# The first inverse moved among the last projections, and a hand-written order for TensorE in the recurrence stage

## The chip, the cores and the metric

One core of one Trainium2 chip runs the kernel. The metric is device time in microseconds (us) of one execution. Profile and trace come from one execution that the hardware profiler recorded.

## The reference, cut to what matters

Two transformer blocks on 512 tokens of width 1024. The change lies in the first block, whose mixing part has two branches on the same normalised input: a gated delta rule with 8 heads of 64 features, worked in chunks, and a sliding-window attention with 8 query heads.

```python
A = jnp.where(strict, jnp.einsum('bhncd,bhnsd->bhncs', kb, k) * decay, 0.0)
L = A + jnp.eye(CHUNK, dtype=A.dtype)
sol = lax.linalg.triangular_solve(L, rhs, left_side=True, lower=True, unit_diagonal=True)
u, w = sol[..., :Dv], sol[..., Dv:]
qk = jnp.where(causal, jnp.einsum('bhncd,bhnsd->bhncs', q, k) * decay, 0.0)
...
def step(S, inp):
    u_c, w_c, qk_c, qd_c, kd_c, dec_c = inp
    v_new = u_c - jnp.einsum('bhcd,bhde->bhce', w_c, S)
    o = jnp.einsum('bhcd,bhde->bhce', qd_c, S) + jnp.einsum('bhcs,bhse->bhce', qk_c, v_new)
    S = S * dec_c[..., None, None] + jnp.einsum('bhcd,bhce->bhde', kd_c, v_new)
    return S, o
```

After the mixing come the output projection, a feed-forward part, and a second block with four branches; the change does not touch them.

## The kernel before

Features lie on partitions for the projections (weights split into a high and a low float32r part, three matmuls for one product, `mm3`, L302), tokens for the rest. The kernel works the delta rule in 4 chunks of 128 tokens; a chunk is a block `b`, the heads go by parity `e`, so a tile `[P, 512]` holds the four heads of one parity.

The stage that the change is about runs after the queries, keys and values of the delta rule. Its parts:

- **Last projections.** `proj(19 + j)` (four query tiles of the attention) and `gate_z(p)` (L919, four gate tiles), 24 dense 128x512 matmuls each.
- **Inverse of a chunk** (`inverse`, L775). From the inverses of 16x16 diagonal blocks (`block_inverse`, L749) it doubles the block size twice. For each parity there are four products of whole 128x128 matrices, four heads each: L804 and L809 for blocks of 16, L818 and L824 for blocks of 32. VectorE masks or subtracts after the first two, ScalarE copies the kept parts after the last two. It also forms the decayed scores (L796, contraction over 64 partitions). In the trace a float32 matmul is two records, so a product of four heads is eight.
- **Recurrence of a chunk** (`recur`, L847). Keys times state (L836 in `state_product`), then the inverse applied by halves with 64x64 matmuls (L864, L869, L872), then the new state (L880). After each of them VectorE or ScalarE forms the next operand.
- **Outputs of a chunk** (`outputs`, L891). Queries times state (L836), scores times new values (L900), a norm on VectorE and ScalarE, transposes (L916).
- **Attention.** Eight units (4 blocks x 2 key heads). `swa_scores` (L1002): score matmuls L1012, softmax on VectorE and ScalarE. `swa_values` (L1038): transposes L1047, copies on ScalarE, value matmuls L1051.
- **Modulation vectors.** `adaln2` (L366) loads weights on SP's queue, multiplies on ScalarE and adds on GpSimd, then transposes on TensorE (L380) and sums on ScalarE. Two of the six groups stand in this stage.

What sets the order: a planner sorts each engine's instructions by priority and its own estimate of when they are ready. The program gives the turns (L31) and raises the priority of inverse, recurrence and outputs:

```python
TURNS = (0, 0, 1, 1, 0, 2, 1, 2, 3, 2, 3, 3)
...
    with tc.high_priority(offset=1000):
        done = next(steps[b], "done") == "done"
```

Engines take their instructions in the planned order, and an instruction that waits holds those behind it. PSUM has eight banks (L239): here 0, 1, 2 for the inverse, 4 for the recurrence, 5 for the outputs, 3 and 7 for attention scores and transposes, 6 for attention values and the modulation vectors.

Earlier, `conv_silu` (L603) takes twelve projection tiles through a causal convolution: ScalarE copies the tile from PSUM to SBUF (L607), scales it once more from PSUM (L610), and VectorE adds the three other taps from the SBUF copy (L612).

Of the kernel before, what the change touches and what calls it, by code (L numbers as in the profile page):

```python
# [16 lines left out]
P = 128  # L17
T = 512
# [10 lines left out]
ADA_AT = (2, (3, 4), (3, 6))  # L29
# [21 lines left out]
# column offsets in the packed table of per-feature vectors  # L51
# [9 lines left out]
# columns of the constant table  # L61
# [32 lines left out]
def _rope():  # L94
    """rows 0-63 ones, 64-95 cos, 96-127 signed sin, for the 528 positions; then the row map of the key rotation."""
    inv = (1.0 / (10000.0 ** (np.arange(0, 32, 2, dtype=np.float32) / np.float32(32)))).astype(np.float32)
    ang = np.arange(TM, dtype=np.float32)[None, :] * inv[:, None]
    cos, sin = np.cos(ang).astype(np.float32), np.sin(ang).astype(np.float32)
    t = np.zeros((P, TM + P), np.float32)
    t[:64, :TM] = 1.0  # L100
    t[64:96, :TM] = np.concatenate([cos, cos])
    t[96:, :TM] = np.concatenate([-sin, sin])
    i = np.arange(32)
    for a_ in (64, 96):
        for b_ in (64, 96):
            t[a_ + i, TM + b_ + i] = 1.0
    return t


def _pack(inp):  # L110
# [13 lines left out]
    # shift1 | scale1 by feature tile, then the other four by 512 columns  # L124
# [87 lines left out]
class Halves:  # L212
    """a weight chunk [P, 8, 128] kept as two tiles [P, 512]"""
# [9 lines left out]
def build(ctx, tc, A, out):  # L223
    nc = tc.nc
    V, S, G, E = nc.vector, nc.scalar, nc.gpsimd, nc.tensor
# [71 lines left out]
    def mm3(dst, w, wk, x, first=True, last=True):  # L297
        """dst += W^T x over the k-tiles: wk are positions in the weight chunk, x the (hi, lo) operands."""
# [14 lines left out]
    def gemv(how, acc, views, after=None):  # L313
        """acc [P, n] = sum over the k-tiles of weights times silu(c); by VectorE, or ScalarE and GpSimd."""
# [18 lines left out]
    def early_slots():  # L333
        """tiles [P, 512] in space that is free until the projections are under way"""
# [15 lines left out]
    def adaln1(k, how, raws, after=None):  # L350
        """shift1 and scale1 of feature tile k"""
# [14 lines left out]
    def adaln2(g, how, ring):  # L366
        """modulation tiles 16 + 4g to 19 + 4g"""
# [9 lines left out]
        gemv(how, acc, views)  # L377
        pt = psum("sm")
# [6 lines left out]
        V.tensor_tensor(out=mod[:, c:c + 4], in0=mod[:, c:c + 4], in1=vec[:, VEC["b_ada"] + c:VEC["b_ada"] + c + 4], op=ALU.add)  # L385

# [5 lines left out]
    def rsqrt(t, w, sfx=""):  # L392
        """t <- t^-0.5 in place, t a 2D [p, w] view: bit-level first guess and three Newton steps."""
# [15 lines left out]
    def rms_stat(tiles, n, width=T, scratch=work):  # L409
        """rstd with tokens on partitions, [P, blocks], and the last matmul on its way"""  # L410
# [17 lines left out]
    def rms_spread(rs, width=T):  # L428
        """rstd by token along the free axis on all partitions, [P, width] in PSUM"""
# [10 lines left out]
    def modulated(xt, bc, w, sh, sc, hh, hl):  # L440
        """h = x*rstd*w*(1+scale)+shift for one feature tile, split."""
# [63 lines left out]
    def spare_w(i):  # L505
        """weights in the slots that the scores take later"""
# [21 lines left out]
    def tr4(src, dst):  # L528
        """transpose the four 128x128 blocks of src [P, 512] into the PSUM tile dst."""
# [45 lines left out]
    # decays to the end of the chunk: of the keys, and of the state by parity of the head  # L575
# [7 lines left out]
    # G along the free axis on all partitions, by way of DRAM  # L583
# [19 lines left out]
    def conv_silu(i, ct_, dst):  # L603
        """projection tile i -> causal conv (channel tile ct_) -> silu, into dst [P, 512]."""
        pt = proj(i)
        raw = xtile(turn[0] % 2)
        S.activation(out=raw, in_=pt, func=AF.Copy)  # L607
# [3 lines left out]
        for j in (1, 2, 3):  # L611
            V.scalar_tensor_tensor(out=y[:, j:T], in0=raw[:, 0:T - j], scalar=wj(3 - j), in1=y[:, j:T],  # L612
# [10 lines left out]
    def kstat(pt, dst, scale):  # L623
        """dst [P, NB, 2] = (sum of squares per head * scale + eps)^-0.5, from PSUM with tokens on partitions."""
# [16 lines left out]
    def head_sums(src, dst, p):  # L641
        """sums of squares of the heads 2p and 2p + 1 into dst [P, (chunk head)]"""
# [13 lines left out]
    def key_scales():  # L656
        """rk: sums of squares, the factor beta / sum, and the norm"""
# [7 lines left out]
    def key_rows(p):  # L665
        """keys by token, decayed to the end of the chunk"""
# [33 lines left out]
    rot = {"n": 0}  # L700

    def tmp_tile(b):
        if b == 0:
            return work()
        rot["n"] += 1
        return htile(f"l{4 + rot['n'] % 4}")
# [19 lines left out]
    def key_products(b, e):  # L726
        """at = Gram products of the keys times factor and decay; their 32x32 diagonal blocks to c32 [P, (chunk head), 32]"""
# [21 lines left out]
    def block_inverse():  # L749
        """x16 [P, (chunk head), 16]: the inverses of the 16x16 diagonal blocks by substitution, columns on partitions."""  # L750
# [6 lines left out]
        # sel[:, j]: row j of every block for all rows of the block  # L757
# [16 lines left out]

    def inverse(b):  # L775
        """Zi[b, e] = transpose of (I + A)^-1 for heads 2q + e, by doubling the block size; qkT[b, e] the decayed scores.
        Yields between the steps, so that two chunks can take turns."""
        at, x = {}, {}
        s = slice(b * P, (b + 1) * P)
        cs = [slice(q * P, (q + 1) * P) for q in range(4)]  # L780
        for e in range(2):
            i = 2 * (b % 2) + e
            o = 64 * e
            dt = qkT[b, e]
            at[e] = Zf[b, e]
            z = Zi[b, e] = (xtile(6 + e) if b == 0 else htile(f"h{i}") if b == 1 else
                            htile(f"h{e}") if b == 2 else gp.tile([P, T], F32, tag="Z", name="Z", bufs=8))
# [3 lines left out]
            x[e] = (gs.tile([P, T], F32, tag="vn", name="x", bufs=2) if b == 0 else  # L791
                    htile(f"h{4 + i}" if b < 2 else f"l{i}"))
# [939 lines left out]
```

## Time and profile before

| | us |
|---|---|
| median of 3 runs | 1276.18 |
| lowest and highest | 1273.61, 1287.78 |
| the profiled execution, first to last instruction (span) | 1298.0 |

The profiled execution is longer than each of the timed runs although its span leaves out what lies around the instructions. TensorE's granted clock, over the whole span, was 0.965 of full speed. The last projections end and the stage of inverse, recurrence and attention takes over near 216 us of the span; the output projection starts at 351 us, and the recurrence of the last chunk runs on among its products to 386 us.

How to read the rows: times are us from the start of the span. A stage's row has the busy time of PE (TensorE matmul), PEld (its weight loads), DVE (VectorE), ACT (ScalarE) and POOL (GpSimd), and the granted clock of TensorE as a share of full speed (1.00 is 2.4 GHz, 0.50 is 1.2 GHz).

### The profile page before, as it was taken

To read this page: it belongs to the slowest core of one execution; us is meant where nothing else is said; L and a number is where in the kernel's file an instruction comes from. 1 tells how busy PE (TensorE), PEld (TensorE's weight loads), DVE (VectorE), ACT (ScalarE), POOL (GpSimd) and SP (SyncE) were. 2 spreads that over 40 slices of the span, in tenths; PEclk is the share of its full clock that TensorE was granted. 3 is DMA by queue.
4 is the path that set the end of the run, shared out by engine and by line. 5 is a ranking of instruction groups with operands and counts; after the bars stand their busy time and mean duration, and the time that the engine had idled before them with its cause. 6 is when DMAs were issued, how large, how long until landed. Compare 5 with 4: busy or idle time off the path is not lost.

```text
span 1298.0 us, 17212 instructions
## 1 busy us (share of the span) xinstructions
PE 1253.2 (97%) x6470; PEld 1034.5 (80%) x6470; DVE 827.1 (64%) x1694; ACT 542.6 (42%) x1098; POOL 118.8 (9%) x99
## 2 busy tenths in 40 slices
PE   4989999999999999999999999999999999999997
PEld 4767778767799888888888889888888888788876
DVE  7789989554766643334433336798778876754554
ACT  5467733544635332222232223444444454432341
POOL 3450334310000000000000000012000000000000
PEclk9899999765999999999999999899999999999999
DMA  9545433210231423333233335122222222232441
GB/s 356 181 127 155 138 97 106 90 33 17 66 99 50 165 95 98 97 98 97 87 104 106 106 110 152 49 76 88 69 78 82 62 81 78 65 106 94 137 144 49
DMA packets 52627, 132.63 MB, mean 102 GB/s; under 512 B 6560, under 2 KB 14272, under 8 KB 52544
## 3 DMA queue, kind: packets, MB, share of 16 engines
q1 hardware_dynamic: 49472, 126.21, 30.8%
q10 hardware_dynamic: 3072, 5.33, 1.2%
q8 instruction: 51, 0.84, 0.3%
q14 instruction: 32, 0.26, 0.1%
HBM read 127.30 MB, written 4.21 MB: 101 GB/s over the span
## 4 chain that ended last, share of the span: by engine, by line
PE 82%; DVE 10%; DMA 5%; ACT 2%; issue 1%; POOL 0%; SPq 0%; DVEq 0%; ACTq 0%; POOLq 0%
PE ps_mm L302 56%; PE ps_out L302 4%; DVE x L612 2%; PE ps_ff L302 2%; DMA ada<-in_ada 2%; PE ps_po L1051 1%; PE ps_swa L1012 1%; PE ps_sc L1545 1%; DVE wlo L284 1%; PE ps_o L1575 1%; DMA raw<-in_wo 1%; PE ps_mm L1690 1%; PE ps_mm L1691 1%; PE ps_tr L1569 1%; PE ps_mm L1689 1%
## 5 line engine op out<-in xcount | busy, mean ns | idle before, releaser
L283 ACT ACTIVATE whi<-raw 128x1024 fp32r<-128x1024 f32 x141 | 147.3, 1045 | 268.9 <-PE ps_mm L302 206.2
L284 DVE TENSOR_TENSOR wlo<-raw,whi 128x1024 fp32r<-128x1024 f32 x140 | 170.9, 1221 | 94.9 <-ACT whi L283 94.6
L302 PE MATMUL ps_mm<-uh,whi 128*128 128x512 f32 (+1 forms) x544 | 197.3, 363 | 0.0
L302 PE MATMUL ps_mm<-uh,wlo 128*128 128x512 f32 (+1 forms) x544 | 196.7, 362 | 0.5 <-DVE work L1279 0.4
L302 PE MATMUL ps_mm<-ul,whi 128*128 128x512 f32 (+1 forms) x544 | 195.4, 359 | 0.0
L302 PE MATMUL ps_mm<-mh,whi 128*128 128x512 f32 x320 | 126.3, 395 | 0.0
L302 PE MATMUL ps_mm<-mh,wlo 128*128 128x512 f32 x320 | 125.2, 392 | 0.3 <-DVE wlo L284 0.3
L302 PE MATMUL ps_mm<-ml,whi 128*128 128x512 f32 x320 | 125.5, 392 | 0.0
L302 PEld LDWEIGHTS ps_mm<-ul,whi 128*128 128x128 f32 x544 | 102.5, 188 | 15.7 <-issue 0.7
L302 PEld LDWEIGHTS ps_mm<-uh,wlo 128*128 128x128 f32 x544 | 102.3, 188 | 15.8 <-DVE work L1279 0.7
L302 PEld LDWEIGHTS ps_mm<-uh,whi 128*128 128x128 f32 x544 | 102.3, 188 | 15.7 <-issue 1.5
L302 PEld LDWEIGHTS ps_mm<-ml,whi 128*128 128x128 f32 x320 | 60.0, 188 | 14.2
L302 PEld LDWEIGHTS ps_mm<-mh,wlo 128*128 128x128 f32 x320 | 60.0, 188 | 14.1 <-DVE wlo L284 0.4
L302 PEld LDWEIGHTS ps_mm<-mh,whi 128*128 128x128 f32 x320 | 59.9, 187 | 13.4
L302 PE MATMUL ps_mm<-ah,whi 128*128 128x512 f32 x176 | 69.8, 396 | 0.0
L302 PE MATMUL ps_mm<-ah,wlo 128*128 128x512 f32 x176 | 69.8, 396 | 0.0
L302 PE MATMUL ps_mm<-al,whi 128*128 128x512 f32 x176 | 69.8, 396 | 0.0
L302 PE MATMUL ps_mm<-hh,wlo 128*128 128x512 f32 x144 | 59.2, 411 | 0.6 <-ACT x L969 0.4
L329 POOL TENSOR_TENSOR acc<-acc,ada 128x512 f32<-128x512 f32 (+1 forms) x42 | 51.3, 1222 | 87.7 <-ACT ada L328 74.4
L302 PE MATMUL ps_mm<-hl,whi 128*128 128x512 f32 x144 | 59.3, 412 | 0.0
L302 PE MATMUL ps_mm<-hh,whi 128*128 128x512 f32 x144 | 59.2, 411 | 0.0
L1193 DVE SCALAR_TENSOR_TENSOR fa<-th,ps_mm 128x512 f32<-128x512 f32 x20 | 13.8, 688 | 58.2 <-ACT th L1191 58.2
(565 smaller groups left out, 2570.0 us busy)
## 6 DMA issues: line engine op xcount, KB each, us to landing
raw<-in_win SPq DMA_DIRECT2D x80, 512.0 KB, 3.6
ada<-in_ada SPq DMA_DIRECT2D x48, 256.0 KB, 5.5
raw<-in_wgate SPq DMA_DIRECT2D x22, 512.0 KB, 3.5
raw<-in_wup SPq DMA_DIRECT2D x22, 512.0 KB, 3.5
ada<-in_ada SPq DMA_DIRECT2D x16, 512.0 KB, 3.7
raw<-in_wdown SPq DMA_DIRECT2D x16, 512.0 KB, 3.5
x<-in_xT SPq DMA_DIRECT2D x16, 256.0 KB, 4.2
raw<-in_wout SPq DMA_DIRECT2D x8, 512.0 KB, 3.5
```

The lines of the kernel that those rows point to most:

```text
L283: S.activation(out=hi[:, 0:n, :], in_=raw[:, 0:n, :], func=AF.Copy)
L284: eng.tensor_tensor(out=lo[:, 0:n, :], in0=raw[:, 0:n, :], in1=hi[:, 0:n, :].bitcast(F32), op=ALU.subtract)
L302: E.matmul(dst, ww[:, k, :], xx, start=first and i == 0, stop=last and i == len(seq) - 1)
L329: G.tensor_tensor(out=acc, in0=acc, in1=src, op=ALU.add)
L612: V.scalar_tensor_tensor(out=y[:, j:T], in0=raw[:, 0:T - j], scalar=wj(3 - j), in1=y[:, j:T], op0=ALU.mult, op1=ALU.add)
L1012: E.matmul(pp[:, f + c0_:f + 256], qsT[j][o:o + 64, b * P:(b + 1) * P], ksT[o:o + 64, k0:(b + 1) * P], start=True, stop=True)
L1051: E.matmul(po_[o:o + 64, :], Vs[:, kblk * P + o:kblk * P + o + 64], pT, start=kb == kbs[0], stop=kb == 1)
L1193: V.scalar_tensor_tensor(out=fa, in0=th, scalar=1.0, in1=pg, op0=ALU.add, op1=ALU.mult)
L1545: E.matmul(pt[:, 0:w], xx[:, sl_], kk[:, c], start=q == 0, stop=q == 2)
L1569: E.transpose(pt[0:nk, i * P:(i + 1) * P], pv(i, c), ident)
L1575: E.matmul(po_[:, w], vhl[b][0:nk, P * hd:P * hd + P], xx[0:nk, w], start=b == 0 and q == 0, stop=b == NB and q == 1)
L1689: E.matmul(po_, ml[:, sl_], wh[:, c], start=k == 0, stop=False)
```

## The change

- `conv_silu`: the copy L607 is gone; VectorE's three taps read the projection from PSUM.
- The first chunk's inverse (steps `i0`) and its decayed scores (`d0`) are issued among the four query projections and the four gate projections (`DENSE`), at raised priority.
- After that every TensorE instruction of the stage gets an ordering dependency on the one before (`Ordered.strict`, `CHAIN`): `r` recurrence, `i` inverse of chunks 1 to 3, `d` decayed scores, `o` outputs, `s` one of 24 attention steps, `a` one of two steps of a modulation group. The attention, whose scores of the first units stood among the projections, starts inside this order, after `r0`.
- The inverse's products are taken by two 64x64 diagonal blocks per head in place of one 128x128 matrix, the lower and the upper block by turns. VectorE's mask and subtraction go by halves: two instructions on 64 partitions for one on 128.
- Decayed scores and `state_product` alternate the two parities, each in its own PSUM bank.
- Banks: 0 and 1 inverse and outputs' `state_product`; 4 and 5 recurrence; 2 outputs; 6 attention values and modulation.

The output projection behind the stage is not in the strict order; the planner places it.

```diff
-TURNS = (0, 0, 1, 1, 0, 2, 1, 2, 3, 2, 3, 3)
+DENSE = ("Q0", "i0", "Q1", "i0", "Q2", "i0", "Q3", "i0", "z0", "i0", "z1", "d0", "z2", "z3")
+CHAIN = ("r0", "i1", "s", "a4", "r0", "i1", "s", "r0", "i1", "s", "r0", "i1", "s", "s", "r1", "i1",
+         "s", "r1", "d1", "s", "s", "r1", "o0", "i2", "s", "r1", "i2", "s", "s", "r1", "i2", "s",
+         "r2", "i2", "s", "a4", "i2", "s", "a5", "o0", "r2", "d2", "s", "r2", "o1", "s", "i3", "r2",
+         "i3", "s", "r2", "i3", "s", "r3", "i3", "s", "a5", "i3", "s", "o1", "r3", "d3", "s", "r3",
+         "o2", "s", "r3", "s", "o2", "s", "o3", "o3")
...
+        def put(self, ins):
+            if self.strict and self.last is not None:
+                tc.add_manual_dep(ins.ins, self.last.ins.name, NOSYNC, reason="order")
+            self.last = ins
+            return ins
...
     def conv_silu(i, ct_, dst):
         pt = proj(i)
-        raw = xtile(turn[0] % 2)
-        S.activation(out=raw, in_=pt, func=AF.Copy)
...
-            V.scalar_tensor_tensor(out=y[:, j:T], in0=raw[:, 0:T - j], scalar=wj(3 - j), in1=y[:, j:T],
+            V.scalar_tensor_tensor(out=y[:, j:T], in0=pt[:, 0:T - j], scalar=wj(3 - j), in1=y[:, j:T],
...
+    def decayed(b):
+        s = slice(b * P, (b + 1) * P)
+        qk = [psum(stream_of(b)) for _ in range(2)]
+        for q in range(4):
+            for e in range(2):
+                o = 64 * e
+                E.matmul(qk[e][:, q * P:(q + 1) * P], kT[q][o:o + 64, s], qT[q][o:o + 64, s], start=True, stop=True)
+        for e in range(2):
+            V.tensor_tensor(out=qkT[b, e], in0=qk[e], in1=qkT[b, e], op=ALU.mult)
...
+        def products(dst, left, right):
+            for q in range(4):
+                for r in ends:
+                    c = slice(q * P + r.start, q * P + r.stop)
+                    E.matmul(dst[r, c], left[r, c], right[r, c], start=True, stop=True)
...
+        pp, pj = [psum(stream) for _ in range(2)], []
+        for e in range(2):
+            products(pp[e], at[e], x[e])
+            pj.append(work())
+            for r in ends:
+                V.tensor_tensor(out=a3(pj[e])[r, :, r], in0=a3(pp[e])[r, :, r],
+                                in1=bcm(cc("lev", P))[r, :, r], op=ALU.mult)
+        yield
...
     def state_product(dst, xT_, St, b, stream):
+        pk = [psum(stream) for _ in range(2)]
...
+        for q in range(4):
+            for e in range(2):
+                o = 64 * e
+                E.matmul(pk[e][:, q * 64:(q + 1) * 64], xT_[q][o:o + 64, b * P:(b + 1) * P], St[o:o + 64, q, :],
+                         start=True, stop=True)
...
-        pa = psum("inv")
+        yield
+        pa = psum("rec")
...
-            state_product(on, qT, St, b, "so")
+            state_product(on, qT, St, b, "inv")
...
+    banks["sm"] = (6, 7)
+    for name in DENSE:
+        step(name)
+    banks.update({"inv": (0, 1), "rec": (4, 5), "so": (2,), "sm": (6,)})
+    E.strict, E.last = True, None
+    for name in CHAIN:
+        step(name)
+    E.strict = False
```

## Rows read from the trace of the kernel before

**Rows 1.** The page: TensorE's busy time, and its granted clock in 40 slices.

```profile
PE 1253.2 (97%) x6470; PEld 1034.5 (80%) x6470; DVE 827.1 (64%) x1694; ACT 542.6 (42%) x1098; POOL 118.8 (9%) x99
PEclk9899999765999999999999999899999999999999
```

**Rows 2.** Busy time by stretch: PE, PEld, DVE, ACT, POOL, clock, DMA.

```profile
216.00:240.00 24.00, 21.36 (x165) 18.45 (x164) 19.49 (x51) 13.97 (x42) 10.44 (x8) 1.00 0.36 110
240.00:261.00 21.00, 20.80 (x103) 16.31 (x102) 9.27 (x18) 9.64 (x27) 6.55 (x6) 0.51 0.24 76
261.00:271.00 10.00, 7.67 (x65) 5.96 (x63) 7.55 (x22) 5.42 (x16) 3.14 (x3) 1.00 0.26 79
271.00:319.00 48.00, 48.00 (x198) 35.34 (x197) 20.50 (x58) 19.71 (x69) 1.26 (x1) 0.50 0.05 17
319.00:351.00 32.00, 32.00 (x245) 24.23 (x245) 25.12 (x72) 21.13 (x67) 0.00 (x0) 1.00 0.11 34
```

**Rows 3.** The same view, single stretches ahead of or at a lower clock.

```profile
85.00:90.00 5.00, 2.76 (x15) 2.07 (x15) 5.00 (x6) 3.05 (x5) 3.61 (x3) 1.00 0.22 80
90.00:95.00 5.00, 5.00 (x20) 3.87 (x19) 3.27 (x5) 3.45 (x10) 2.48 (x2) 0.66 0.00 0
...
235.00:240.00 5.00, 3.11 (x26) 2.31 (x26) 1.12 (x4) 4.91 (x18) 1.26 (x1) 1.00 0.31 99
```

**Rows 4.** Timeline of PE just ahead of the clock's two returns: start, us, instruction.

```profile
257.78 3.50 PE L824 MATMUL ps_inv<-h,blank 128*128 128x128 f32 x16
...
314.66 1.91 PE L818 MATMUL ps_inv<-l,Z 128*128 128x128 f32 x8
```

**Rows 5.** Chain of work in order of time, pieces at half clock: start, us, what.

```profile
253.20 3.60 PE ps_so L900 x16
...
276.89 2.00 PE ps_swa L1012 x4
278.90 1.89 PE ps_inv L869 x16
```

**Rows 6.** The same view, pieces at full clock.

```profile
268.52 1.16 PE ps_inv L796 x8
...
325.61 1.09 PE ps_inv L809 x8
...
328.54 1.07 PE ps_inv L869 x16
...
330.61 1.06 PE ps_swa L1012 x4
...
334.82 0.89 PE ps_inv L804 x8
...
340.38 0.61 PE ps_rec L880 x16
341.00 1.93 PE ps_so L900 x16
...
343.59 1.03 PE ps_rec L836 x8
...
346.92 1.86 PE ps_po L1051 x4
348.77 0.81 PE ps_swa L1047 x6
```

**Rows 7.** Timeline of PE at half clock: L836 by turns and alone.

```profile
302.12 0.42 PE L836 MATMUL ps_so<-St,qT 64*128 64x64 f32 x1
302.18 0.42 PE L836 MATMUL ps_rec<-St,kT 64*128 64x64 f32 x1
302.33 0.42 PE L836 MATMUL ps_so<-St,qT 64*128 64x64 f32 x1
...
309.92 1.11 PE L836 MATMUL ps_rec<-St,kT 64*128 64x64 f32 x4
```

**Rows 8.** Groups from 60 to 165 us, ACT then DVE: busy, mean ns, idle.

```profile
L607 ACT ACTIVATE x<-ps_mm 128x512 f32<-128x512 f32 x12 | 7.0, 582 | 0.0
...
L612 DVE SCALAR_TENSOR_TENSOR x<-x,hconv,x 128x511 f32<-128x511 f32 (+2 forms) x36 | 33.7, 954 | 1.3 <-ACT x L610 1.3
```

More of the change, by code (lines that the diff above doesn't have):

```diff
@@ L224, in build, with matmul, transpose @@
     nc = tc.nc
-    V, S, G, E = nc.vector, nc.scalar, nc.gpsimd, nc.tensor
+    V, S, G = nc.vector, nc.scalar, nc.gpsimd
+    class Ordered:
+        strict, last = False, None
+        def put(self, ins):
[3 more added lines that the diff above has]
+            return ins
+        def matmul(self, *a, **k):
+            return self.put(nc.tensor.matmul(*a, **k))
+        def transpose(self, *a, **k):
+            return self.put(nc.tensor.transpose(*a, **k))
+    E = Ordered()
     scope = [ctx]
@@ L385, in adaln2 @@
         V.tensor_tensor(out=mod[:, c:c + 4], in0=mod[:, c:c + 4], in1=vec[:, VEC["b_ada"] + c:VEC["b_ada"] + c + 4], op=ALU.add)
+        yield
+    def adaln2(g, how, ring):
+        for _ in adaln2_steps(g, how, ring):
+            pass
     accp = pool("accp", 2)
@@ L698, in htile @@
         return hm.tile([P, TM], F32, tag=tag, name=tag)[:, 0:T]
[L700 to L706, printed above, removed]
     def decay(b, e):
@@ L797, in inverse @@
-            V.tensor_tensor(out=dt, in0=qk, in1=dt, op=ALU.mult)
         yield
+        pp, pj = [psum(stream) for _ in range(2)], []
[5 more added lines that the diff above has]
+                                in1=bcm(cc("lev", P))[r, :, r], op=ALU.mult)
+        yield
+        pz = [psum(stream) for _ in range(2)]
         for e in range(2):
@@ L801, in inverse @@
             z = Zi[b, e]
-            pp = psum("g" if b == 0 else "inv")
-            for c in cs:
-                E.matmul(pp[:, c], at[e][:, c], x[e][:, c], start=True, stop=True)
-            pj = tmp_tile(b)
-            V.tensor_tensor(out=a3(pj), in0=a3(pp), in1=bcm(cc("lev", P)), op=ALU.mult)
-            pz = psum("g" if b == 0 else "inv")
-            for c in cs:
-                E.matmul(pz[:, c], pj[:, c], z[:, c], start=True, stop=True)
-            V.tensor_tensor(out=z, in0=z, in1=pz, op=ALU.subtract)
+            products(pz[e], pj[e], z)
@@ L811, in inverse @@
+            for r in ends:
+                V.tensor_tensor(out=a3(z)[r, :, r], in0=a3(z)[r, :, r], in1=a3(pz[e])[r, :, r], op=ALU.subtract)
             V.transpose(out=x[e], in_=z)
         yield
+        pp = [psum(stream) for _ in range(2)]
+        for e in range(2):
+            products(pp[e], at[e], x[e])
+            for o in (0, 64):
+                S.activation(out=a3(blank[e])[o + 32:o + 64, :, o:o + 32], in_=a3(pp[e])[o + 32:o + 64, :, o:o + 32], func=AF.Copy)
+        yield
+        pz = [psum(stream) for _ in range(2)]
@@ L814, in inverse @@
         for e in range(2):
             z = a3(Zi[b, e])
-            pp = psum("g" if b == 0 else "inv")
-            for c in cs:
-                E.matmul(pp[:, c], at[e][:, c], x[e][:, c], start=True, stop=True)
-            pj = blank[e]
+            products(pz[e], blank[e], Zi[b, e])
             for o in (0, 64):
-                S.activation(out=a3(pj)[o + 32:o + 64, :, o:o + 32], in_=a3(pp)[o + 32:o + 64, :, o:o + 32], func=AF.Copy)
-            pz = psum("g" if b == 0 else "inv")
-            for c in cs:
-                E.matmul(pz[:, c], pj[:, c], Zi[b, e][:, c], start=True, stop=True)
@@ L988, in build, with swa_query @@
     rqs = sw.tile([P, 4, NB, 2], F32, name="rqs")
-    for j in range(4):
+    def swa_query(j):
         pt = proj(19 + j)
@@ L998, in build @@
         V.tensor_tensor(out=rqs[:, j, :, :], in0=rqs[:, j, :, :], in1=isl, op=ALU.mult)
-    for p in range(4):
-        gate_z(p)
     def swa_scores(b, kv):
@@ L1070, in build, with step @@
     ring_x = lambda: [xtile(4), xtile(5)]
-    for n, b in enumerate(TURNS):
-        if n <= len(swa_units):
-            swa_step(n)
-        if n in ADA_AT[2]:
-            adaln2(2 + len(ADA_AT[1]) + ADA_AT[2].index(n), "A", ring_x)
-        with tc.high_priority(offset=1000):
-            done = next(steps[b], "done") == "done"
-        if done:
-            for f in (recur, outputs):
-                with tc.high_priority(offset=1000):
-                    f(b)
+    running = {("s", 0): swa_steps()}
+    for g in (4, 5):
+        running["a", g] = adaln2_steps(g, "A", ring_x)
+    for b in range(NB):
+        running["i", b], running["r", b], running["o", b] = steps[b], recur(b), outputs(b)
+    def step(name):
+        kind, i = name[0], int(name[1:] or 0)
+        if kind == "Q":
+            swa_query(i)
+        elif kind == "z":
+            gate_z(i)
+        else:
+            with tc.high_priority(offset={"r": 2000, "s": 0, "a": 0}.get(kind, 1000)):
+                if kind == "d":
+                    decayed(i)
+                else:
+                    next(running[kind, i], None)
+    banks["sm"] = (6, 7)
[6 more added lines that the diff above has]
+    E.strict = False
     mixed = [(hm.tile([P, TM], F32R, tag=f"h{p}", name="mh")[:, 0:T], hm.tile([P, TM], F32R, tag=f"l{p}", name="ml")[:, 0:T])
```

96 lines of the change are left out of this document (49 added, 47 removed).

## The prediction, made before the changed kernel ran

> **What bounds the kernel now.** I read four views: the page for the whole, the stretches of the changed stage, then the timeline and the chain of waits inside it for prices. The page says that TensorE (PE) is busy for 1253 of 1298 us and that its granted clock is near full except in slices 8 to 10 [rows 1]. Those slices are the changed stage. Resolved into stretches, PE idles little there: 24.00 - 21.36 = 2.6 us, 0.2 us and 2.3 us up to 271 us, then nothing, 5 us in all [rows 2]. But from 240 to 261 and from 271 to 319 us it ran at 1.2 GHz, half of full speed, while its busy time was the whole stretch [rows 2]. VectorE was busy for 20.50 of the 48 us of the longer one. So the stage is bound by PE at half clock, and the question is what the change does to PE's work and to its clock.
>
> What did PE do before the clock fell or rose? It fell after stretches with gaps: 2.76 busy of 5 us before the fall at 90 us, 3.11 of 5 before the one at 240 us [rows 3]. The fall at 271 us follows 7.67 busy of 10 us [rows 2]. It came back each time right after back-to-back products with the full 128x128 array: 3.50 us of L824 before 261 us, and L818 and its neighbours before 319 us [rows 4]. It did not come back through 48 us of unbroken work [rows 2] that was mostly attention scores and values and 64x64 or 64x128 matmuls, which use half or a quarter of the array. In this trace, then, a busy PE was not enough to get the clock back; full-array products did it.
>
> **PE's work, part by part, at full clock.** Prices are the pieces of [rows 6].
>
> Inverse: 4 chunks x 2 parities x 4 products are 32 groups of 8 records, 0.89 to 1.09 us each, 0.99 taken: 31.7 us removed. Each becomes 16 records of 64x64. Bounds: 1.07 us if they run one behind the other, as L869's 16 do (all in one corner of the array), and 0.61 us if two run at once, as L880's 16 do, whose outputs alternate between the two halves of the partitions. The new blocks differ in rows and columns of the array, so 0.61 is nearest: 32 x 0.61 = 19.5 us, a gain of 12 (bounds: a loss of 2.5, a gain of 12).
>
> Decayed scores: 8 groups of 1.16 us = 9.3; `state_product`: 12 groups of 1.03 us = 12.4. With the parities by turns I take half. The lower bound is no gain. For the gain the trace has a precedent: where L836 of the outputs and of the recurrence happened to alternate, a pair took 0.21 us (302.12 to 302.33), against 1.11 / 4 = 0.28 for one record alone [rows 7]. Gain 4.7 + 6.2 = 11.
>
> Sum: 12 + 11 = 23 us of PE work less, at full clock.
>
> What is left in the strict order, at full clock: products 24 x 0.61 = 14.6; decayed scores 3.5; `state_product` 6.2; L864, L869 and L872 12 x 1.07 = 12.8; L880 1.8; L900 4 x 1.93 = 7.7; attention scores 12 x 1.06 and 2.1 for the first block's, half as wide, = 14.8; values 28 x 0.465 = 13.0; transposes (56 of L1047, 24 of L916 and L380) 80 x 0.135 = 10.8. Together 85 us. The first inverse and its scores, 8 x 0.61 + 1.2 = 6 us, go among dense projections at full clock. So the stage has 91 us of work, and before it had 91 + 23 = 114.
>
> **The clock.** The same pieces at half clock: 1.89 against 1.07 us, 2.00 against 1.06, 3.60 against 1.93 [rows 5, 6], a factor of 1.85. Before, 69 us at half clock [rows 2] did 69 / 1.85 = 37 us of work: 32 us lost. 114 + 32 + 5 idle = 151 us for the stage.
>
> After, all 128x128 products are gone from the order, the very work that brought the clock back. What stays is quarter- and half-array work, L900, and short runs of transposes. And the fall comes early: the attention now starts after `r0`, so its first transposes stand in the strict order behind a softmax that nothing has hidden yet, and everything behind them (recurrence, inverse, outputs) waits on PE's queue too. I expect the clock to fall after some 6 us of the 85, and to return only when the planner sets the output projection's dense products among the last 12 us of work, as it did before. 85 - 6 - 12 = 67 us at half clock cost 0.85 x 67 = 57 us more.
>
> **Waits.** Idle before was 5 us [rows 2]. At half clock the other engines have time, but the strict order adds waits: for the first softmax, and twice at `a`, whose transposes now share bank 6 with the attention values and so wait for their copies. I take double, 10 us; bounds 5 and 27, the latter the 2.6 us of the worst gap ahead of ScalarE [rows 2] at each of ten turns. VectorE's 16 more instructions (halves of mask and subtraction) cost at most 16 x 0.95 = 15 us of its time [rows 8] and lie in the half that it idles at half clock; at full clock they would not be covered. The modulation groups keep their loads, ring and engines; SP's queue behind them holds the output projection's weights, as before.
>
> **`conv_silu`.** Twelve copies, 7.0 us of ScalarE, go [rows 8]. Where PE waited most in this part (2.76 busy of 5 us at 85 to 90) VectorE was full [rows 3], and its taps take 954 ns on average [rows 8]. Reading from PSUM they may be quicker; the PSUM bank is held longer, though, until the third tap. I take a gain of 4 us: of the 2.2 us gap, the 1.7 us lost at clock 0.66 right after it [rows 3], and little else. Bounds: nothing, and 10.
>
> **Sum.** Against the profiled execution: 91 + 57 + 10 = 158 against 151, less 4: 3 us more, 1301 for a span of 1298. Against the runs it is not the same sum. The profiled span is 22 us over their median of 1276, and what varies most between executions must be the clock, since the gaps that made it fall are small; the runs themselves differ by 14 us. I ascribe 12 of the 22 us to the clock, so that the median run lost 32 - 12 = 20 us. The change's loss hangs on no such luck. 1276 - 23 + (57 - 20) + 5 - 4 = **1291 us**. With none of the 22 ascribed it would be 1279, with all of them 1301; with the long waits 1308. Own range 1279 to 1308.
>
> **Rivals.**
>
> *The clock holds* (the other side). The order by turns was to keep PE fed: an attention step stands behind nearly every dependent step. If no gap like the one at 235 us [rows 3] opens early, PE keeps 2.4 GHz and VectorE, 82 us busy from 216 to 351 us [rows 2], becomes as long as PE. Then 91 + 16 us of waits = 107, against 114 + 20 + 5 = 139 in the median run: 1276 - 32 - 4 = **1240**. For it: from 319 to 351 us PE held 1.00 with mixed work and no idle time [rows 2]. Against: that stretch still had L804 and L809 in it [rows 6]. It decides as soon as the first softmax is hidden. The Trainium skill ("TensorE: Matmul & The Clock Gate", section "Why this matters for your kernels") speaks for this rival: it asks that there be no long idle gaps between bursts of matmuls, and then the clock stays up. By that rule a strict order without gaps would give 1240; the trace differs in one point, since at 271 to 319 us there was no gap and the clock stayed down.
>
> *The clock comes back midway.* Half of the 57 us: **1263**. For it: transposes and L900 are full-array too, and a run of both might do. Against: they never stand together for as long as L824 did [rows 4].
>
> *The blocks don't run at once.* Then the products cost 1.07 per group: 8 x 0.46 in the projections, and some 24 x 0.46 in the order, mostly times 1.85, 22 us more: **1313**. For it: no matmul of before uses two opposite corners of the array. Against: L880 and L836 both overlapped [rows 6, 7].
>
> **How the numbers follow.** Chances: the forecast 0.55, clock holds 0.22, clock back midway 0.15, no overlap 0.08. About 1% (13 us) is what a measurement of this kernel can tell from no change, so the bounds are 1263 and 1289. Faster: the clock that holds, and half of midway, 0.29. Same: the other half, and the lower third of the forecast, 0.26. Slower: the rest, 0.45. The range reaches from 1243, which leaves out half of the first rival (0.11), to 1311, which leaves out most of the last (0.06).
>
> **What would show it.** Clock: one stretch at 0.50 from near 220 us to the output projection, with PE busy throughout; a clock at 1.00 there, or one that returns before the first output product, makes me wrong, and the time then goes to 1240 or 1263. Pieces: 16 records of 64x64 in 0.6 us at full or 1.05 at half clock; 1.07 or 1.89 means no overlap. Waits: idle PE near 10 us between 216 us and the output projection, most of it early, ended by ScalarE's softmax. `conv_silu`: PE busy over 2.76 of 5 us near 85 us, taps shorter than 954 ns.

## The result, and the profile after

The kernel after takes 1311.0 us (median of 4 runs, 1303.9 to 1320.5) against 1275.8: a ratio of 1.027, 95% interval 1.020 to 1.034. It is slower, as the forecast's likeliest case had it, but by 35 us and not by 15. The profiled execution took 1316.6 us with a span of 1314.5; 2 us lie around the span.

The page of after, TensorE's busy time and the granted clock in 40 slices, to be laid beside [rows 1]:

```profile
PE 1242.5 (95%) x6726; PEld 1024.7 (78%) x6726; DVE 824.6 (63%) x1710; ACT 537.9 (41%) x1086; POOL 118.4 (9%) x99
PEclk9898997667589999999999999999999999999999
```

The low slices are now 7 to 11. The same stretch cut where the clock changes (busy time of each engine, clock, DMA share), to be laid beside [rows 2]; the fourth, sixth and last row each hold one or more short falls:

```profile
core 0: us, PE busy (x) PEld busy (x) DVE busy (x) ACT busy (x) POOL busy (x), PEclk, DMA share, GB/s
215.40:242.70 27.30, 24.73 (x247) 20.95 (x248) 18.91 (x53) 15.61 (x44) 13.78 (x11) 0.50 0.40 126
242.70:249.50 6.80, 4.39 (x60) 3.82 (x60) 5.56 (x12) 3.63 (x10) 3.85 (x4) 1.00 0.38 106
249.50:280.30 30.80, 24.25 (x135) 17.48 (x135) 11.89 (x34) 15.73 (x45) 3.79 (x3) 0.50 0.12 37
280.30:300.70 20.40, 14.95 (x166) 9.98 (x166) 13.57 (x40) 9.69 (x38) 0.00 (x0) 0.92 0.00 1
300.70:317.80 17.10, 17.05 (x94) 13.17 (x95) 8.34 (x23) 7.36 (x20) 0.00 (x0) 0.50 0.19 56
317.80:338.30 20.50, 13.98 (x179) 9.85 (x179) 14.18 (x38) 9.35 (x29) 0.00 (x0) 0.83 0.13 36
338.30:362.20 23.90, 23.90 (x140) 18.36 (x137) 14.06 (x38) 11.39 (x37) 0.00 (x0) 0.50 0.12 41
362.20:425.60 63.40, 57.05 (x453) 53.79 (x452) 36.57 (x98) 22.07 (x52) 0.00 (x0) 0.95 0.26 76
```

From the last projection to the last output product the kernel before took 192.0 us (215.8 to 407.8) and after takes 215.5 (210.0 to 425.6). TensorE's work there, added up from the time between the starts of its matmuls and brought to full clock, fell from 152.7 to 129.0 us; its idle time rose from 5 to 34 us; what half clock took, counted as half of the time at half clock, rose from 34 to 58 us. In after some 6 of the 58 fall on idle time and so stand in both terms. The profiled execution of before lost 45 us to the clock over the whole kernel (1298.0 us at 0.965), where the median run lost 20 (table below), so its 34 are more than usual.

The longest waits of TensorE in this stretch (waited for, total, times, longest):

```profile
PE ps_rec L246 <- ACT h L865: 10.6, 4, 8.1
PE ps_sm L246 <- DVE rsy L436: 4.3, 1, 4.3
PE ps_out L246 <- DVE x L1181: 3.7, 1, 3.7
PE ps_inv L246 <- DVE smx L1071: 3.5, 1, 3.5
PE ps_sm L249 <- ACT x L1110: 3.2, 2, 2.2
```

The first wait comes before the set order starts. The last projection ends at 210.4 us, and the second half of the first inverse's products is not ready, since VectorE is still at its subtractions and transposes. TensorE stands for 4.25 us, the clock falls at 215.4 and stays low for 27.3 us, and the rest of the first inverse and its scores run at half clock (start, duration, operation; idle before it in brackets):

```profile
214.69 1.87 PE L246 MATMUL ps_sm<-x,Z 64*64 64x64 f32 x32 [4.25 <-DVE rsy L436]
219.54 2.07 PE L246 MATMUL ps_sm<-qT,kT 64*128 64x128 f32 x8
```

The longest one, on TensorE's timeline:

```profile
245.36 1.15 PE L246 MATMUL ps_inv<-h,blank 64*64 64x64 f32 x32
246.44 0.66 PE L249 MATMUL ps_swa<-cst,sc 128*128 128x128 f32 x4
255.20 0.47 PE L246 MATMUL ps_rec<-tt,h 64*64 64x64 f32 x2 [8.10 <-ACT h L865]
256.53 1.75 PE L246 MATMUL ps_rec<-tt,h 64*64 64x64 f32 x14 [0.86 <-ACT h L865]
258.20 2.08 PE L246 MATMUL ps_inv<-qT,kT 64*128 64x128 f32 x16
```

and ScalarE in the same time:

```profile
247.09 0.72 ACT L354 ACTIVATE x<-x,cact 128x512 f32<-128x512 f32 x1 [0.86 <-DMA x<-in_ada]
250.35 0.72 ACT L354 ACTIVATE x<-x,cact 128x512 f32<-128x512 f32 x1 [2.54 <-DMA x<-in_ada]
252.07 0.72 ACT L354 ACTIVATE x<-x,cact 128x512 f32<-128x512 f32 x1 [1.00 <-DMA x<-in_ada]
254.88 0.56 ACT L865 ACTIVATE h<-ps_inv 32x128 f32<-32x128 f32 x2
```

The inverse's products were ready at 246.5. The copy that the recurrence needs (L865) stood on ScalarE's queue behind sums of a modulation group, which waited for loads, and behind a softmax (252.70 to 254.67 us). In the set order nothing else may pass, so TensorE stood for 8.10 us, and the clock fell at 249.5. It came back at 280.3.

**What the runs say of the clock.** Each run gives its mean granted clock. For the kernel before, 70 runs lie between 1270.8 and 1302.3 us; time multiplied by mean clock lies between 1250 and 1262 in all of them. So most of what differs between its executions is the clock. For every kernel the time is split this way below: us at full clock (time x clock), and us lost to the clock (the rest). Medians of the runs that are compared; executions over 1.5% above the fastest of their kernel are left out of comparisons, which takes three of no_strict's four runs (1314 to 1315 us, clock 0.941) and two of blocks_only's five (1313 and 1315, 0.950 and 0.948).

| kernel | us | clock | at full clock | lost | ratio to before (95%) |
|---|---|---|---|---|---|
| before | 1276.9 | 0.984 | 1256 | 20 | |
| after | 1311.0 | 0.954 | 1251 | 61 | 1.027 (1.020 to 1.034) |
| whole_strict | 1288.0 | 0.978 | 1259 | 28 | 1.012 (1.008 to 1.016) |
| no_strict | 1293.6 (one run) | 0.961 | 1243 | 50 | |
| blocks_only | 1285.0 | 0.967 | 1246 | 42 | 1.007 (1.004 to 1.010) |
| whole_free | 1285.4 | 0.979 | 1259 | 27 | 1.007 (1.005 to 1.009) |
| filler | 1310.0 | 0.970 | 1270 | 40 | 1.026 (1.023 to 1.029) |
| filler_quarter | 1323.8 | 0.970 | 1286 | 39 | 1.035 (1.030 to 1.039) |
| no_mod | 1296.0 | 0.960 | 1246 | 53 | 1.017 (1.013 to 1.020) |
| wide_ring | 1286.6 | 0.978 | 1257 | 28 | 1.008 (1.006 to 1.011) |
| wide_free | 1286.3 | 0.980 | 1259 | 26 | 1.009 (1.006 to 1.013) |
| conv_only | 1278.7 | 0.981 | 1255 | 24 | 1.001 (0.999 to 1.003) |
| conv_ring | 1275.1 | 0.982 | 1253 | 22 | 1.000 (0.998 to 1.002) |
| state_pairs | 1284.2 | 0.982 | 1260 | 22 | 1.005 (1.003 to 1.007) |

After against before: 5 us less at full clock, 41 us more lost.

### The profile page after: what moved, and what is told of

Its sections match the earlier page's. It is cut to its first block, busy times and chain, and to the rows that moved or that the text cites. A ratio compares the mean times of both kernels' runs of the same rounds, so it can differ in the third digit from the quotient of the medians.

```text
span 1314.5 us, 17753 instructions
## 1 busy us (share of the span) xinstructions
PE 1242.5 (95%) x6726; PEld 1024.7 (78%) x6726; DVE 824.6 (63%) x1710; ACT 537.9 (41%) x1086; POOL 118.4 (9%) x99
## 4 chain that ended last, share of the span: by engine, by line
PE 70%; DVE 5%; DMA 3%; ACT 3%; issue 1%; POOL 1%; SPq 0%; DVEq 0%; ACTq 0%; POOLq 0%
PE ps_mm L246 52%; PE ps_out L246 3%; PE ps_sc L246 2%; PE ps_ff L246 2%; PE ps_rec L246 2%; PE ps_po L246 1%; PE ps_inv L246 1%; DMA raw<-in_wo 1%; PE ps_swa L246 1%; PE ps_o L246 1%; PE ps_so L246 1%; PE ps_tr L249 1%; DVE wlo L310 1%; PE ps_sm L246 1%; PE ps_g L246 1%
```

## The experiments

Two theories to begin with. C: the 64-block products took away the work that keeps the clock up. W: the set order puts all of TensorE behind each late operation of another engine.

**whole_strict: the set order, with whole products.**

```
-            for q in range(4):
-                for r in ends:
-                    c = slice(q * P + r.start, q * P + r.stop)
-                    E.matmul(dst[r, c], left[r, c], right[r, c], ...)
+            for q in range(4):
+                c = slice(q * P, q * P + P)
+                E.matmul(dst[:, c], left[:, c], right[:, c], ...)
```

The mask and the subtraction are on whole tiles again.

> The kernel after, set order kept, with whole 128x128 products in the inverses (and the mask and the subtraction on whole tiles), as the kernel before had them. Theory C: the full-array products bring the clock back where after has half clock; half-clock stretches of the stage fall from 116 us toward the 68 of before, which is 24 us of clock regained for 12 us more of matmuls at full clock: about 1299. Theory W: the waits stay as they are, 12 us at full clock and up to 24 at half are added: 1320 to 1335, and the half-clock stretches stay near 116 us.

Measured: 1288.0 us, 23 less than after, although TensorE has more to do: 8 us more at full clock, 33 less lost. Theory C gave the sign; the gain is larger than the 12 us that it gave. Stretches and TensorE's timeline:

```profile
234.70:244.90 10.20, 6.63 (x37) 5.45 (x38) 1.82 (x6) 8.75 (x32) 3.39 (x4) 0.50 0.32 104
244.90:255.10 10.20, 6.84 (x56) 5.42 (x55) 5.65 (x12) 3.80 (x10) 6.06 (x5) 1.00 0.31 104
258.60:333.60 75.00, 66.74 (x561) 52.24 (x560) 59.94 (x170) 48.73 (x154) 1.27 (x1) 1.00 0.16 49
```

```profile
237.84 0.77 PE L249 MATMUL ps_swa<-cst,sc 128*128 128x128 f32 x2 [7.83 <-ACT sc L321]
240.79 3.78 PE L246 MATMUL ps_inv<-h,Z 128*128 128x128 f32 x16
```

It too has a long gap, 7.83 us, and the clock falls in it, at 234.7. But whole products follow (3.78 us of them), and the clock is back after 10 us, not after 31; from 258.6 it stays up for 75 us. Its idle time in the stage is 26 us, against 34 for after, and its work 145.9 us against 129.0: of the 17 us that the blocks save, 8 come back as idle time.

**blocks_only: the kernel before, with 64-block products** (the loop above, the other way round, in `inverse` of before; mask and subtraction by halves).

> The kernel before with the 64-block products in the inverses alone, and the mask and the subtraction by halves (the planner's order and the turns stay). Theory C: 12 us of matmuls at full clock go, but the full-array products that brought the clock back go with them: half-clock stretches of the stage grow from 68 us to 100 and more, and the time is 1276 to 1292. Theory W: without the set order there is no new wait, and the 12 us, at half clock up to 16, are gained: 1258 to 1266.

Measured: 1285.0 us, 8 more than before: 10 less at full clock (12 forecast), 22 more lost. Theory C, and neither the set order nor its waits are needed for it. In the profiled execution (1313 us) it went furthest:

```profile
205.00:226.70 21.70, 18.58 (x167) 14.14 (x165) 20.84 (x73) 6.34 (x9) 9.70 (x8) 1.00 0.35 108
226.70:339.40 112.70, 109.24 (x668) 80.55 (x668) 57.55 (x158) 50.90 (x157) 17.53 (x15) 0.50 0.15 46
```

After 2.9 us of waiting for VectorE at 223.4, the clock stayed at half for 112.7 us, with TensorE busy for 109.24 of them.

**no_strict: after, in the planner's order.** `E.strict` stays False.

> The kernel after without the set order: the same matmuls, the planner orders them, each engine still runs in order. Theory W (the set order's waits are the loss; they are about 34 us of the stage where before had 5): most of the 29 us more of waiting goes and the clock has fewer gaps to fall after, about 1285 (1278 to 1292). Theory C (the quarter-array matmuls alone keep the clock low, whatever their order): half clock for 100 us and more of the stage as in after, and no more than 10 us gained, 1300 to 1311.

Measured: TensorE's idle time in the stage fell from 34 to 14 us, and the time at full clock by 8 us, to 1243, as W has it. But the time, 1293.6 us in one run and 1314 to 1315 in three, bears out neither forecast: the first lies between them, the others above both. The clock is the reason, here in the run of 1293.6:

```profile
214.00:265.20 51.20, 49.28 (x406) 40.94 (x403) 30.13 (x83) 25.30 (x65) 21.31 (x17) 0.50 0.33 104
```

With 1.9 us idle in 51 it ran at half clock. As in after, the fall came behind a wait of the first inverse for VectorE, 3.62 us up to 212.78. Also, the pairs of scores came apart: the planner put them parity by parity, 8 records in 2.07 us at half clock, where the set order has 16 in 2.08 (above, at 258.20):

```profile
246.76 2.07 PE L246 MATMUL ps_inv<-qT,kT 64*128 64x128 f32 x8
```

**whole_free: whole products and the planner's order** (both edits above).

> The kernel after with whole 128x128 products in the inverses and without the set order: what is left of the change is the pairs (scores, state products), the recurrence by pieces, the earlier first inverse and the convolution. Theory C (full-array products keep the clock, the planner's order has few waits): the time at full clock is that of whole_strict, 1288 x 0.978 = 1260, less some 10 us of the waits that the set order has, 1250; with half clock as before (mean clock 0.984) 1270 (1262 to 1278), the best of all. Rival (the planner's order mixes quarter-array and half-array work in long stretches, and loses the clock also with whole products): 1285 or more.

Measured: 1285.4 us, the rival's side of the forecast by its time, but not by its reason: clock and time at full clock are those of whole_strict (0.979, 1259). What the planner saves in waits (idle 17 us against 26) it gives back in work (152.6 us against 145.9); the pairs of scores come apart here too, 8 records in 1.16 us.

**filler: after, with full-array work added.** The results of the added matmuls aren't used.

```
         def products(dst, left, right):
+            for q in range(2):
+                E.matmul(dst[:, q * P:(q + 1) * P], ident, ident, start=True, stop=True)
             for q in range(4):
```

> The kernel after, 64-block products kept, with two full 128x128 matmuls of the identity in front of each parity's eight block products, into the columns that these write next (work added, its result unused). TensorE has the same time to work as in whole_strict. Theory C (it is the share of full-array work that sets the clock, not the shape of the products as such): the half-clock stretches go as in whole_strict and the time falls in spite of 17 us more of matmuls: 1282 to 1296. Rival (the block products lose the clock by their own shape, or the waits do): the 17 us come on top, at full or half clock: 1325 to 1345.

**filler_quarter: the same with quarter-array work.**

```
+            for q in range(8):
+                for r in ends:
+                    c = slice(q % 4 * P + r.start, q % 4 * P + r.stop)
+                    E.matmul(dst[r, c], ident[r, r], ident[r, r], start=True, stop=True)
```

> The kernel after with sixteen 64x64 matmuls of the identity in front of each parity's block products, in place of filler's two full 128x128 ones: the same 17 us of added TensorE time, but quarter-array (work added, its result unused). Theory C (the share of full-array work sets the clock): the clock stays at after's mean of 0.954 or falls, and 17 us at full clock cost 17 to 30: 1328 to 1341. Rival (any added work that fills TensorE's time lifts the clock, as it did in filler): 1306 to 1314, mean clock 0.969.

Measured: both have a mean clock of 0.970, against 0.954. filler costs 19 us at full clock and gets 21 back, so its time is that of after: between the two forecasts. filler_quarter costs 35 at full clock (its added blocks also pushed the end of the projections from 210 to 228 us) and gets 22 back, so its time lies between its two forecasts too, with the mean clock that the rival gave. So theory C as first put falls: it isn't the share of full-array work. TensorE's timeline of filler_quarter shows it directly:

```profile
236.37 1.91 PE L246 MATMUL ps_inv<-cst 64*64 64x64 f32 x32 [0.70 <-DVE work L845]
238.00 1.13 PE L246 MATMUL ps_inv<-h,work 64*64 64x64 f32 x16
238.86 1.61 PE L246 MATMUL ps_inv<-cst 64*64 64x64 f32 x32
240.27 0.66 PE L246 MATMUL ps_inv<-h,work 64*64 64x64 f32 x16
```

and the stretches:

```profile
236.50:239.90 3.40, 3.40 (x68) 3.40 (x69) 3.34 (x11) 0.00 (x0) 1.58 (x2) 0.50 0.65 199
239.90:243.30 3.40, 1.03 (x34) 0.89 (x31) 2.73 (x12) 3.22 (x15) 1.26 (x1) 1.00 0.49 160
```

The clock, low since 236.5, came back at 239.9, and TensorE had run nothing but 64x64 blocks in between. In after it came back seven times before the output projection (242.7, 280.3, 293.9, 317.8, 334.9, 362.2 and 369.0 us), each time behind value products, which use half of the array, with at most 1.1 us of other work between. The return at 280.3:

```profile
274.74 1.96 PE L246 MATMUL ps_inv<-l,Z 64*64 64x64 f32 x29
276.62 3.67 PE L246 MATMUL ps_po<-pT,Vs 128*64 128x512 f32 x4
```

What is left of C: taking work out of this stage takes the clock with it, and putting work in, of either kind, gives it back. That the added work filled the gaps is not the reason: TensorE's idle time is 36 us in both fillers against 34 in after, and the longest gap 8.3 and 11.3 us, while half clock took 22 and 26 us of the stage against 58. Value products alone do not settle it either: those at 260.2 us in after did not bring the clock back. Why 51 us of nearly unbroken mixed work in no_strict did not, stays open.

**no_mod: after, without the last two modulation groups.** Left out: their loads, sums and transposes; eight columns of the modulation are zero.

> The kernel after without the last two modulation groups (their loads, ScalarE sums and transposes are left out, eight columns of the modulation are zero instead), set order and 64-blocks kept. Theory W (late ScalarE and loads of these groups, which hold up the set order, are the loss): the waits of the recurrence on the copy of the inverse (8.1 us longest) and of the group's transposes (3.2 us) go, and the clock's falls behind them: 1285 to 1298. Theory C: the waits go, but the quarter-array work stays, and the clock stays low in about the same share of the stage: 1300 to 1311.

Measured: 1296.0 us, 15 less than after (5 at full clock, 8 lost, the rest lies between the medians); near the upper end of W's range. The long wait is gone, but the idle time of the stage is 33 us as before; other waits took its place:

```profile
PE ps_rec L246 <- ACT h L865: 4.7, 2, 2.8
PE ps_sm L246 <- DVE rsy L436: 4.3, 1, 4.3
PE ps_inv L246 <- DVE l L851: 3.7, 2, 2.7
PE ps_so L249 <- DVE on L959: 3.6, 1, 3.6
```

So the groups' loads choose where TensorE waits, and hardly how long in all.

**wide_ring and wide_free: six slots for these loads, not two**, in whole_strict and in whole_free.

```
-    ring_x = lambda: [xtile(4), xtile(5)]
+        return [htile(("h4", "h5", "l4", "l5", "l6", "l7")[(six[0] + i) % 6]) for i in range(2)]
```

> As whole_strict (whole products, set order), with six slots in place of two for the loads of the last two modulation groups, so that their sums wait less for loads. Theory W (the set order loses its time to ScalarE work that stands behind late loads): TensorE's waits in the stage fall from 24 us to 14, the time at full clock from 1260 to 1250, and at whole_strict's mean clock of 0.977 the time from 1288 to 1278 (1272 to 1284). Rival (ScalarE's sums now come earlier and stand in front of the copies of the inverse instead): 1285 to 1292, no gain.

> As whole_free (whole products, planner's order), with the six slots. Where the chain of loads holds the stage, its waits of 15 us fall to 8: 1279 (1272 to 1284) against 1286 for whole_free. Where it does not: 1283 to 1290.

Measured: 1286.6 and 1286.3 us, no gain in either. wide_ring's longest wait is still 7.4 us for ScalarE's scaling of the scores (7.8 in whole_strict), and its idle time 27 us. In wide_free the idle time fell from 17 to 12 us, but the time at full clock stayed at 1259. Slots for loads are not the bound.

**conv_only: the kernel before, with the convolution's change alone.**

```
-        raw = xtile(turn[0] % 2)
-        S.activation(out=raw, in_=pt, func=AF.Copy)
-            V.scalar_tensor_tensor(out=y[:, j:T], in0=raw[:, 0:T - j], ...
+            V.scalar_tensor_tensor(out=y[:, j:T], in0=pt[:, 0:T - j], ...
```

> The kernel before with the convolution's change alone (no raw copy, the taps read the projection's bank). Theory of the forecast: 4 us less, about 1272. Rival: the bank is held for the three taps, TensorE waits for it before the next projection as it does for 6.2 us in the profile of after, and the gain is eaten up: 1274 to 1280.

Measured: no difference (1278.7 us, the rival's side). The taps' mean fell from 954 ns [rows 8] to 742, and TensorE waited for them, where it had waited 1.5 us for ScalarE before. The taps' group (count, busy us and mean ns, idle before), and the wait:

```profile
L610 DVE SCALAR_TENSOR_TENSOR x<-ps_mm,hconv,x 128x511 f32<-128x511 f32 (+2 forms) x36 | 26.4, 742 | 2.8 <-ACT x L608 2.7
```

```profile
PE ps_mm L302 <- DVE x L610: 6.8, 2, 5.6
```

The mean of 954 hides two sizes. The source view of before and of conv_only has the shortest, median and longest tap in ns:

```profile
L612 DVE SCALAR_TENSOR_TENSOR x<-x,hconv,x x36: 734/746/1803, 70.9 to 152.4; 128x511 f32<-128x511 f32 x12, 128x510 f32<-128x510 f32 x12, 128x509 f32<-128x509 f32 x12
L610 DVE SCALAR_TENSOR_TENSOR x<-ps_mm,hconv,x x36: 734/742/751, 65.3 to 144.9; 128x511 f32<-128x511 f32 x12, 128x510 f32<-128x510 f32 x12, 128x509 f32<-128x509 f32 x12
```

From SBUF 28 of the 36 taps take 734 to 752 ns, as from PSUM. The other eight take 1165 to 1803, and all eight ran while GpSimd added up a modulation vector, as here (DVE and POOL timelines of before):

```profile
80.33 1.78 DVE L612 SCALAR_TENSOR_TENSOR x<-x,hconv,x 128x511 f32<-128x511 f32 x1
78.87 4.40 POOL L329 TENSOR_TENSOR acc<-acc,ada 128x512 f32<-128x512 f32 x3 [4.98 <-DVE wlo L284]
```

Of the taps from PSUM several ran beside GpSimd too, and none took longer than 751 ns.

In the two profiled executions the last projection starts at 211.7 us, less 8.5 for its half-clock stretches, against 215.8 less 6.9: 5.7 us earlier. The stage behind it, at full clock, is longer by about as much (164.7 against 157.9 us): TensorE's work there is 156.2 us against 152.7, and its idle time 9 against 5.

**conv_ring: conv_only with four slots for the modulation loads**, since conv_only's chain of work ran through them.

> The kernel before with the convolution's change and four slots in place of two for the loads of the last two modulation groups. In conv_only the last projections end about 5 us earlier and the stage behind is 5 us longer at full clock; its chain runs through these loads. If the loads take the gain away, four slots give it back: 1270 (1266 to 1274), faster than before. If the gain is lost in another way (TensorE's work in another order, ScalarE): 1275 to 1282.

Measured: a ratio of 1.000. The loads don't take the gain away. TensorE's work in the stage is 157.1 us here, against 152.7 in before for the same matmuls, so what is lost is lost mostly in how its matmuls follow each other; why the planner's order got worse isn't found.

**state_pairs: conv_ring with the state products of both parities by turns**, in the planner's order.

```
+        pk = [psum("rec"), psum("so")]
+        for q in range(4):
+            for e in range(2):
+                E.matmul(pk[e][:, q * 64:(q + 1) * 64], xT_[q][o:o + 64, ...], St[o:o + 64, q, :], ...)
```

> conv_ring with the state products of the two parities by turns into two banks, nothing else of the change (5.6 us of TensorE's time at full clock less, all of it half-array work; the full-array products stay). If TensorE's work is the bound of the stage: 1275 - 5 = 1270 (1266 to 1272), faster than the kernel before. If the waits of the stage take it back, as whole_free suggests (pairs, and no gain): 1274 to 1280.

Measured: 1284.2 us, 0.5% slower, above both forecasts. The edit didn't do what it says: the planner took the pairs apart, 8 records of one parity at the full 1.10 us, so no work was saved (157.4 us, conv_ring 157.1), and TensorE waited more (idle 15 us against 7.5), for a reason that is not shown:

```profile
270.43 1.10 PE L834 MATMUL ps_so<-St,qT 64*128 64x64 f32 x8
291.55 1.10 PE L834 MATMUL ps_rec<-St,qT 64*128 64x64 f32 x8
```

No version beat the kernel before; conv_ring equals it.

## Why the prediction was right, and where it was not

The direction was right, the time 20 us short: 1311.0 lies 3 us above the forecast's own range of 1279 to 1308, and at the very end of the range over all its cases. In the forecast's terms: 1276 - 23 (work) + 37 (clock) + 5 (waits) - 4 (convolution) = 1291. Measured: 1276 - 24 + 41 + 23 - 5 = 1311. The 41 is from the table of medians. The 24 and 23 are from the stage in the two profiles (34 us idle against 5 is 29 more, less the 6 that the clock's term already holds). The 5 is what remains. In the profiles it lies ahead of the stage, where after needs 7 us less at full clock (201.5 against 208.9 us up to the last projection).

**TensorE's work: right.** 152.7 to 129.0 us. The blocks overlap: 32 in 1.15 us (above, at 245.36) is 0.57 per group of 16, where 0.61 was taken; the rival without overlap (1.07) is out. The scores' pair, 16 in 2.08 us at half clock, is what was taken. The set order is needed for the scores: without it they came apart in no_strict and whole_free, where the state products of the keys stayed together (16 records in 1.11 us). In state_pairs the state products came apart.

**Waits: the term that was mis-sized.** 10 us forecast, bounds 5 and 27, measured 34 up to the last output product: 4 before 216 us, 25 in the set order, 4 among the output products. The forecast looked for the softmax and for the transposes of `a`, and priced a turn by the worst gap of before, 2.6 us. The wait that mattered was of another kind: ScalarE's queue is in order too, and two copies of 0.56 us together stood there behind sums that waited for loads and behind a softmax, 8.10 us in all. The rows for it were there: ScalarE waiting for these loads cost nothing in before, as TensorE had other work. That the waits are many, and not this one, is shown by no_mod, where it goes and the idle time stays.

**The first inverse: a wait put at nothing.** The forecast laid its 6 us "among dense projections at full clock". The projections ended first: TensorE stood 4.25 us for it, and the clock fell behind that gap, at 215.4 us, before the first softmax that the forecast had made the cause.

**The clock: right in size, wrong in its reason.** Forecast: 57 us lost in the stage; measured 58 in the profiled execution, which lost 70 over the whole kernel where the median run lost 61. That the size fits is partly luck, since the loss is not one stretch from near 220 us to the output projection, as forecast: the clock came back seven times before the output products. The step that failed is the reading of [rows 4], that full-array products bring the clock back. Half-array value products stood before the returns in after, and 64x64 blocks in filler_quarter. The other half of that reading held: a busy TensorE isn't enough (109.24 of 112.7 us in blocks_only). A return before the first output product should have led to 1240 or 1263 by the forecast; it led to 1311, because each return was followed by another gap and another fall. The rival of a clock that comes back midway was so right in what happens and wrong in its price. That taking the whole products out costs clock, on which the forecast's sum rests, is what whole_strict and blocks_only show; the two fillers show that work of either shape gives it back. How the amount of work sets the clock stays open.

**The 22 us between profile and median: mis-sized.** 12 were given to the clock; it was all of them: the profiled execution lost 45 us to the clock, the median run 20. By the text's own sentence that makes 1301.

**The convolution: a gain of 4 forecast, none measured alone** or with more slots; inside the lower bound. What the forecast looked for near 85 us came: TensorE is busy for 3.76 of 5 us there in conv_only, not 2.76, and the clock holds behind it. But the held bank took 5 us of waiting, with half clock from 106.5 to 113.3 us, and the stage grew. The reason that the forecast hoped for, quicker taps from PSUM, is not what the taps show; they lost the delay beside GpSimd. Whether the change is what made after's first part shorter, no run separates.

**The rivals.** The clock that holds (1240) is out: the clock fell at 215.4 us, before the first softmax could decide, and the order left waits of 25 us behind it. The Trainium skill ("TensorE: Matmul & The Clock Gate", section "Why this matters for your kernels") asks for no long idle gaps. Some falls agree: 8.10 us idle around the one at 249.5 us, 7.83 us around whole_strict's at 234.7. Others do not: filler_quarter's at 236.5 us had 0.70 us idle in the 8 us before it. The long low stretches do not follow from it either: no_strict had 1.9 us idle in 51 and stayed at 0.50.

## What to carry to other kernels

Before TensorE's work is cut in a stage that already loses its clock, price the clock with the work: here the whole change took 24 us of work out and lost 41 us more to the clock, and the blocks alone 10 and 22. An order written for one engine is an order for all that feed it; each operand's producer has to be followed on its own queue, down to the loads, since every late one now stops everything. The pairs of scores overlapped only where the order was enforced. Whether enforcing it for the pairs alone, and not for the whole stage, would pay was not tried. A mean over a group of instructions can hide two sizes: look at the shortest and the longest before a price is taken from it.

## What the hardware did that was not expected

- Half clock held through 112.7 us with TensorE busy for 109.24 of them (blocks_only). In filler_quarter it ended behind 64x64 blocks alone.
- Over 70 runs of one kernel, from 1270.8 to 1302.3 us, time x mean clock stayed within 1%.
- VectorE's taps take about 745 ns, from PSUM and from SBUF alike. Eight of 36 from SBUF took 1165 to 1803 ns, all beside a running GpSimd sum; none from PSUM did. The Trainium skill ("VectorE: DVE Perf Modes", section "Rules for kernel authors") leaves two ways for elementwise work on a matmul result: take the slower rate from PSUM, or copy it to SBUF first if many operations follow. For these three taps in float32 no slower rate from PSUM shows (medians 742 and 746 ns), and the time was the same.
- The time of a VectorE operation on the inverse's tiles went by the columns and not by the partitions (mean ns behind the busy time):

```profile
L842 DVE TENSOR_TENSOR work<-ps_inv,csta 64x256 f32<-64x256 f32 x12 | 5.0, 421 | 0.2
L879 DVE TENSOR_TENSOR tt<-ps_rec,egc 128x256 f32<-128x256 f32 x6 | 2.3, 418 | 0.1
L913 DVE TENSOR_TENSOR tt<-tt,ps_rec 64x512 f32<-64x512 f32 x3 | 2.1, 692 | 3.5 <-PE ps_rec L246 3.5
```

  So two half masks of 64x256, which leave out the columns off the diagonal blocks, cost 160 ns more than one whole mask of 128x512 (682 ns in whole_strict).
